# The gate of the last 256 channels of the last 128 tokens goes into their weights; the last multiplication is shared 640 to 384 by ScalarE and VectorE

## The chip, the cores and the metric

The kernel runs on one core of one Trainium2 chip, as one program. The metric is the device time of an execution in microseconds (us). The kernel before takes 963.58 us (median of 3 runs, 963.45 to 964.17). A profile is one further execution with the hardware profiler on; its timeline counts from the start of its span. Engines are TensorE (PE; PEld is its weight load), VectorE (DVE), ScalarE (ACT), GpSimd (POOL) and SyncE (SP), which issues DMA transfers.

## The reference

A decoder trunk of two layers on 1024 tokens of 1024 channels, in float32. The first layer is a gated pooling mixer. The second is sliding-window attention (16 heads of 64, window 128, one sink per head, a shared position bias) with a gate per element; its output goes through a projection `b_w_out`, is multiplied by a gate per channel (from the condition `c`) and added to the stream. A last RMSNorm follows. The change touches only the end of this:

```python
def rmsnorm(x, g):
    y = x * lax.rsqrt(jnp.mean(x * x, axis=-1, keepdims=True) + EPS)
    return y * g

# second layer; y = (o * silu(z)) @ w_out, o the attention's output
x = x + gate[:, None, :] * y
return rmsnorm(x, final_g)
```

Since the gate is one number per output channel, `gate * (a @ w)` equals `a @ (w * gate)`, up to rounding.

## The kernel before, in words

The stream is held transposed: eight tiles `x` of 128 channels by 1024 tokens. Every float32 product is made of three TensorE passes over a high and a low part of each operand (`wh`/`wl` or a pair in `raw` or `wo` for weights); a weight is split by an ACT copy (high) and a DVE subtraction (low).

The second layer (from about L1050) isn't written in the order in which it runs. Each operation is recorded by `note(engine, length, f, reads, writes, lag)` with an assumed length and lag, `in_order` (L1138) simulates the five queues with these numbers and gives the order of all engines, and the instructions are then issued in that order. The waits between engines follow from what the instructions read and write, and each engine works its queue strictly in order. `specs` (L1860 on) lists the work of TensorE: projections of queries and gates, then the output projection, per half `q` of the tokens and per group of heads; `attend` (L1328) puts the attention of a block of 128 tokens between them. An attention block goes: scores on PE (L1354, L1355) into bank `S`; on DVE a masked copy (L1358) and bias, maximum (L1365, four heads); exponentials on ACT (L1369); on DVE the reciprocal (L1376) and the product (L1378); four transposes on PE (L1388) into `tp`; high part on ACT (L1392), low part on DVE (L1393); two masks on POOL (L1400, L1404, giving `pp` and `ph`); four matmuls on PE (L1418, L1419) into `o`; ACT copy `ol` (L1425) and DVE additions (L1431), the gating (L1438) and the split of the result (L1441 on ACT, L1443 on DVE). A tile of the output projection ends on DVE with gate, residual and bank evacuation at once (L696), and then its square on ACT (L1462), summed on POOL (L1467).

The last 128 tokens of the last four heads' part are handled apart. `out_most` multiplies the other 384 tokens of the second half. The weights of that part, `wo` (four pairs, `last_w`), stay in memory. For the last tokens `out_end` (L1576 to L1578) uses the activations as the stationary operand and the weights as the moving one, so that the result has the tokens on partitions, 256 channels for each of four steps `n2`. `turn_last` transposes the stream of these tokens to match (L1553, banks `S`). `rows_in` fetches the gate along a row: SP writes the eight columns `adac[:, 40:48]` to a row in DRAM (L1530) and loads it back broadcast to all partitions (L1536); the final gain row is loaded in the same way. Both go to tiles of the ring `raw1` (two buffers, which the raw weights went through before). `add_end(n2)` then multiplies by the gate (L1592, DVE), adds the stream (L1596, DVE) into `x`, squares with a sum per token (L1599, ACT) and, for `n2` below 2, multiplies by the gain on POOL (L1603). `scale_end` takes the power −1/2 of the mean on POOL (L1622), multiplies the first 512 channels by it on ACT (L1628) and the other 512 by it and the gain on DVE (L1630), and stores each half, from ACT's queue (L1634) and SP's (L1636). The other 384 tokens are scaled by `finish` (L1744 to L1749) and stored from SP (L1753) in the same last microseconds.

## Time and profile before

| what | value |
|---|---|
| time, median of 3 runs | 963.58 us |
| profiled execution, its own time | 965.07 us |
| its span | 963.4 us |
| TensorE busy, its mean granted clock | 953.7 us (99%), 0.997 |
| DVE / ACT / POOL busy | 757.0 / 425.1 / 143.7 us |
| last matmul starts | 956.34 us |
| last stores issued, ACT and SP | 959.71 and 959.91 us |
| gate row: written (L1530), loaded (L1536) | issued at 870.40 and 884.92 us |
| gate row first read | 951.01 us (L1592) |

A row of a timeline gives start, duration, engine, line, operation, output `<-` inputs, shapes, count, and in brackets the idle time of the engine ahead of it and what ended it. The names in it are tiles of the program without buffer numbers; `raw` in a row of a profile stands for `raw1` too. A duration reaches to the result; the next instruction of the same engine can start a little before that, so what an instruction costs its engine is the distance from its start to the next one's. In a DMA row the last number is the time from issue to landing. In a table of stages each engine has its busy time and count, then come the granted TensorE clock, the DMA engines' busy share, and GB/s.

### The profile page before, as it was taken

The page shows a single profiled execution, that of the slowest core. Times are in us where ns is not written, and L with a number is a line of the kernel's source. Part 1 is how long each engine was busy: PE and PEld are TensorE (multiplying, and loading weights), DVE is VectorE, ACT ScalarE, POOL GpSimd, SP SyncE. Part 2 cuts the span into 40 slices and gives each one's busy share as a digit, 9 for nine tenths or more (in the row PEclk, how much of TensorE's full clock was granted, in tenths as well). Part 3 has the DMA queues.
Part 4 walks back from the last instruction along what each step waited for, and adds up shares of the span by engine and source line. Part 5 has one row for each costly group of instructions (what it writes and reads, how often), then busy time and mean ns, then how long its engine had stood idle before and what let it go on. Part 6 is the DMA issues. An engine that isn't in the chain of part 4 may idle for free.

```text
span 963.4 us, 12687 instructions
## 1 busy us (share of the span) xinstructions
PE 953.7 (99%) x4468; PEld 797.0 (83%) x4468; DVE 757.0 (79%) x1414; ACT 425.1 (44%) x872; POOL 143.7 (15%) x229
## 2 busy tenths in 40 slices
PE   9999999999999999999999999999999999999997
PEld 6888888888888887888888888888888888888887
DVE  6999899686978799677755659489999757678785
ACT  6536455332533344551123335366666334455434
POOL 3000000000000000000022200222222334344521
PEclk9999999999999999999999999999999999999999
DMA  9453531354125421788888725845566543448022
GB/s 347 179 176 110 197 132 44 109 184 162 48 93 192 153 66 45 265 282 311 298 303 259 259 98 173 310 150 175 188 231 242 171 148 123 167 136 185 31 88 88
DMA packets 52081, 166.57 MB, mean 173 GB/s; under 512 B 6705, under 2 KB 7857, under 8 KB 51890
## 3 DMA queue, kind: packets, MB, share of 16 engines
q1 hardware_dynamic: 39346, 119.63, 36.0%
q0 software_dynamic: 12240, 44.57, 14.2%
q10 hardware_dynamic: 432, 1.57, 0.5%
q8 instruction: 35, 0.57, 0.2%
q14 instruction: 28, 0.23, 0.1%
HBM read 129.04 MB, written 36.70 MB: 172 GB/s over the span
## 4 chain that ended last, share of the span: by engine, by line
PE 90%; DVE 6%; DMA 2%; issue 1%; ACT 0%; DVEq 0%; ACTq 0%; SPq 0%
PE ps_d L211 12%; PE ps_d L646 11%; PE ps_d L1218 9%; PE ps_d L1219 9%; PE ps_d L1220 9%; PE ps_S L211 8%; PE ps_S L646 5%; PE ps_tp L211 4%; PE ps_tp L646 3%; PE ps_o L211 3%; PE ps_o L646 2%; DVE tmp L546 2%; PE ps_d L373 2%; PE ps_S L1355 2%; PE ps_S L1354 2%; PE ps_tp L1388 1%
## 5 line engine op out<-in xcount | busy, mean ns | idle before, releaser
L211 PE MATMUL ps_d<-gh,wh 128*128 128x512 f32 x224 | 81.9, 389 | 0.0
L238 DVE CUSTOM_DVE_ANT_0 tmp<-tmp,cact,pk 128x1024 f32<-128x1024 f32 x48 | 60.8, 1282 | 24.9 <-DMA tmp<-ada_rest 24.6
L646 PE MATMUL ps_d<-hs,ws 128*128 128x512 f32 x312 | 74.9, 389 | 0.0
L1369 ACT ACTIVATE P<-P,nm 128x129 f32<-128x129 f32 x128 | 50.2, 394 | 45.5 <-DVE nm L1365 45.3
L1218 PE MATMUL ps_d<-hm,wh 128*128 128x512 f32 x176 | 69.5, 395 | 0.0
L1219 PE MATMUL ps_d<-hm,wh 128*128 128x512 f32 x176 | 68.7, 390 | 0.0
L646 PEld LDWEIGHTS ps_d<-hs,ws 128*128 128x128 f32 x312 | 58.6, 188 | 12.1
L1220 PE MATMUL ps_d<-hm,wl 128*128 128x512 f32 x176 | 68.6, 390 | 0.0
L211 PE MATMUL ps_S<-gh,wh 128*128 128x512 f32 x192 | 67.1, 390 | 0.0
L646 PE MATMUL ps_d<-ha,ws 128*128 128x512 f32 x252 | 60.5, 389 | 0.0
L616 ACT CAST ws<-tw 128x512 fp32r<-128x512 f32 x52 | 31.9, 620 | 59.4 <-DVE tw L621 19.1
L646 PEld LDWEIGHTS ps_d<-ha,ws 128*128 128x128 f32 x252 | 47.3, 188 | 9.8
L538 POOL MEMSET tmp<- 128x16 f32 x12 | 1.3, 111 | 328.6 <-DVE adac L238 122.2
L211 PEld LDWEIGHTS ps_d<-gh,wh 128*128 128x128 f32 x224 | 42.1, 188 | 8.7
L126 ACT CAST wh<-raw 128x1024 fp32r<-128x1024 f32 x24 | 25.2, 1050 | 54.0 <-PE ps_d L211 43.8
L546 DVE TENSOR_TENSOR tmp<-tmp 128x1039 f32<-128x1039 f32 (+3 forms) x36 | 44.4, 1234 | 1.0
L211 PE MATMUL ps_d<-gh,wl 128*128 128x512 f32 x112 | 43.6, 389 | 0.0
L211 PEld LDWEIGHTS ps_S<-gh,wh 128*128 128x128 f32 x192 | 35.9, 188 | 7.4
L1431 DVE SCALAR_TENSOR_TENSOR of<-ps_o,ol 64x256 f32<-64x256 f32 x64 | 26.6, 416 | 19.5 <-ACT ol L1425 18.8
L1400 POOL TENSOR_SCALAR_AFFINE_SELECT pp<-ph 128x1024 fp32r<-128x1024 f32 x28 | 30.6, 1095 | 56.8 <-DVE ph L1393 56.7
L1220 PEld LDWEIGHTS ps_d<-hm,wl 128*128 128x128 f32 x176 | 33.0, 188 | 7.1
L1218 PEld LDWEIGHTS ps_d<-hm,wh 128*128 128x128 f32 x176 | 33.1, 188 | 6.2
(354 smaller groups left out, 2632.3 us busy)
## 6 DMA issues: line engine op xcount, KB each, us to landing
tmp<-ada_rest SPq DMA_DIRECT2D x42, 512.0 KB, 4.5
raw<-wa SPq DMA_DIRECT2D x28, 512.0 KB, 3.4
raw<-wao SPq DMA_DIRECT2D x20, 512.0 KB, 5.1
raw<-kw POOLq DMA_DIRECT2D x20, 512.0 KB, 4.4
wh<-kw POOLq DMA_DIRECT2D x19, 512.0 KB, 3.6
wl<-kw POOLq DMA_DIRECT2D x19, 512.0 KB, 4.4
ad<-ada_first SPq DMA_DIRECT2D x16, 512.0 KB, 5.5
x<-xT SPq DMA_DIRECT2D x32, 256.0 KB, 5.8
```

The costliest lines, as they stand in the source:

```text
L126: nc.scalar.copy(out=wh, in_=raw)
L211: mm(p, lhs, acts(k, hl, q), start=start and k == 0 and s == 0, stop=stop and k == n - 1 and s == 2)
L238: nc.vector.tensor_tensor_reduce(out=raw, in0=raw, in1=ca, scale=0.5, scalar=pk[:, bcol:bcol + 1], op0=ALU.mult, op1=ALU.add, accum_out=ad ...
L546: nc.vector.tensor_add(out=nx[:, 2 * s - 1:], in0=cur[:, 2 * s - 1:], in1=cur[:, s - 1:PAD + T - s])
L616: nc.scalar.copy(out=ws[i][:, 0, :], in_=src)
L646: mm(ps, lhs, acts(k, hl), start=start and k == 0 and s == 0, stop=k == 3 and s == 2, skip_group_check=True)
L1218: mm(p, lh, a[0](), start=k == 0, stop=False)
L1219: mm(p, lh, a[1](), start=False, stop=False)
L1220: mm(p, ll, a[0](), start=False, stop=k == n - 1)
L1369: note(ACT, 0.41, lambda: nc.scalar.activation(pt()[:, i, :P + 1], pt()[:, i, :P + 1], AF.Exp, bias=nm()[:, i:i + 1], scale=-1.0, accum_ou ...
L1400: note(POOL, 1.12, lambda: nc.gpsimd.affine_select(out=v8(prev()), in_=v8(cur()).bitcast(F32), pattern=[[0, 8], [-1, P]], base=-1, channel ...
L1431: note(DVE, 0.36, lambda: nc.vector.scalar_tensor_tensor(out=of()[e * 64:(e + 1) * 64, :], in0=o()[0:64, es], scalar=0.5, in1=ol()[0:64, e ...
```

## The change

The raw copy of the last weight pair of the output projection (channels 768 to 1023), which was split for the 384 other tokens as before, is kept in its `raw1` tile. A new step `gate_last`, listed behind the second of the four `out_most`, multiplies it by the gate row (L1570, DVE), and splits the product into a `wl` and a `wh` tile (L1572 on ACT, L1573 on DVE). `out_end(3)` uses that pair. ACT copies the transposed stream of these 256 channels from its bank to memory (L1559), and `add_end(3)` is then one addition of the matmul's result to it (L1618). POOL multiplies channels 512 to 639 by the gain too, ACT's last multiplication takes channels 0 to 639 and DVE's 640 to 1023, and the two stores follow these borders. The gain row goes to the ring `raw`, and the squares go over the tile of the earlier squares instead of a tile of their own.

```diff
-        load("gate", rows[0], [(at, 0)])
-        load("gain", rows[1], ())
+        load("gate", rows[0], [(at, 0)], "raw1", bp, F32)
+        load("gain", rows[1], (), "raw", wp, F32R)
...
-        end["sq"] = tile_of("wh", wp, [P, 1024], F32R, 2)
+        end["sq"] = sqq[0]
...
+        u = end["u"]
+        note(ACT, 0.4, lambda: nc.scalar.copy(
+            out=u().bitcast(F32)[:, 768:], in_=end["bank", 1]()[:, 256:]),
+            [(end["bank", 1], 0)], [(u, 3)])
+
+    def gate_last():
+
+        raw, gate = end["raw"], end["gate"]
+        w = end["w"] = [whole(tile_of(t, wp, [P, 1024], F32R, 2)) for t in ("wl", "wh")]
+        row = lambda: gate()[:, 768:].rearrange("p (i c) -> p i c", i=2).unsqueeze(2).broadcast_to(
+            [P, 2, 4, P])
+        view = lambda: raw().rearrange("p (i k c) -> p i k c", i=2, k=4)
+        note(DVE, 1.2, lambda: nc.vector.tensor_mul(out=view(), in0=view(), in1=row()),
+             [(gate, 0)], [(raw, 0)])
+        note(ACT, 1.0, lambda: nc.scalar.copy(out=w[0](), in_=raw()), [(raw, 0)], w[0].on)
+        note(DVE, 1.16, lambda: nc.vector.tensor_sub(
+            out=w[1](), in0=raw(), in1=w[0]().bitcast(F32)), [(raw, 0)] + w[0].on, w[1].on)
...
-                w = last_w[n2]
+                w = last_w[n2] if n2 < 3 else end["w"]
...
+        else:
+            note(DVE, 0.45, lambda: nc.vector.tensor_add(
+                out=cut("x"), in0=ps()[:, :256], in1=cut("u")), [(ps, 0), (u, n2)], [(x, n2)])
...
-        if n2 < 2:
-            note(POOL, 0.8, lambda: nc.gpsimd.tensor_mul(
-                out=cut("u"), in0=cut("x"), in1=end["gain"]()[:, cs]),
-                [(x, n2), (end["gain"], 0), (state["rs"], 0)], [(u, n2)])
+        if n2 < 3:
+            gs = slice(cs.start, min(cs.stop, 640))
+            of = lambda name: end[name]().bitcast(F32)[:, gs]
+            note(POOL, 0.8 if n2 < 2 else 0.4, lambda: nc.gpsimd.tensor_mul(
+                out=of("u"), in0=of("x"), in1=of("gain")),
+                [(x, n2), (end["gain"], 0), (state["rs"], 0)], [(u, (n2, "a"))])
...
-        note(ACT, 0.6, lambda: nc.scalar.activation(
-            cut("u", 0), cut("u", 0), AF.Copy, scale=rs()[:, 0:1]), [(rs, 0)], [(u, 0), (u, 1)])
+        note(ACT, 0.8, lambda: nc.scalar.activation(
+            cut("u", 0, 640), cut("u", 0, 640), AF.Copy, scale=rs()[:, 0:1]), [(rs, 0)], by_act)
...
-        *[out_most(n2) for n2 in range(4)], bare(turn_last),
+        out_most(0), out_most(1), bare(gate_last), out_most(2), out_most(3), bare(turn_last),
```

The recorded order puts L1570 much earlier than its place in the list. On DVE, in the output projection some 75 us before the end, the order was before (the names are those above; L696 ends a tile of the projection):

```order
L1376 RECIPROCAL den<-den 128x4 [waits Activation_49]
L1378 TENSOR_TENSOR P<-P,den 128x4x128 [waits DVE_49]
L696 SCALAR_TENSOR_TENSOR x<-ps_d,adac,x 128x512 [waits PE_49]
L1443 TENSOR_TENSOR qt<-of,qt 128x2x128 [waits Activation_49]
L696 SCALAR_TENSOR_TENSOR x<-ps_d,adac,x 128x512 [waits PE_49]
L1358 COPY_PREDICATED ps_S<-tri,ps_S 128x2x128 [waits PE_49]
L1393 TENSOR_TENSOR ph<-ps_tp,ph 128x512 [waits Activation_49]
L1358 COPY_PREDICATED ps_S<-tri,ps_S 128x2x128 [waits PE_49]
```

and with the change:

```order
L1376 RECIPROCAL den<-den 128x4 [waits Activation_49]
L1378 TENSOR_TENSOR P<-P,den 128x4x128 [waits DVE_49]
L696 SCALAR_TENSOR_TENSOR x<-ps_d,adac,x 128x512 [waits PE_49]
L1443 TENSOR_TENSOR qt<-of,qt 128x2x128 [waits Activation_49]
L1570 TENSOR_TENSOR raw_7488<-raw_7488,raw_7604 128x1024 [waits DMAHW3_49]
L696 SCALAR_TENSOR_TENSOR x<-ps_d,adac,x 128x512 [waits PE_49]
L1431 SCALAR_TENSOR_TENSOR of<-ps_o,ol 64x256 [waits DVE_49,Activation_49]
L1358 COPY_PREDICATED ps_S<-tri,ps_S 128x2x128 [waits PE_49]
L1393 TENSOR_TENSOR ph<-ps_tp,ph 128x512 [waits Activation_49]
L1358 COPY_PREDICATED ps_S<-tri,ps_S 128x2x128 [waits PE_49]
```

L1570 (raw_7488 is the kept weight tile, raw_7604 the gate row) with its wait for the gate row's DMA stands ahead of the block's third L696 and of the next block's softmax, and one of the two L1431 has come ahead of L1358.

On SP, at the loads of the two rows (raw_7604 and raw_7612 are gate and gain), before:

```order
L1530 DMA row<-adac 128x8x1 [waits DMAHW2_49]
L1536 DMA raw_7604<-row 128x1024 [waits DMAHW2_49,DMAHW3_49,DMAHW0_49,DVE_49]
L1536 DMA raw_7612<-fg_row 128x1024 [waits DMAHW1_49,DVE_49]
L1753 DMA out<-x 128x512 [waits DMAHW5_49,DVE_49]
L1753 DMA out<-x 128x512 [waits DMAHW6_49,DVE_49]
```

and with the change:

```order
L1530 DMA row<-adac 128x8x1 [waits DMAHW2_49]
L1536 DMA raw_7604<-row 128x1024 [waits DMAHW2_49,DMAHW3_49,DMAHW0_49,DVE_49]
L1536 DMA raw<-fg_row 128x1024 [waits DMASW5_49,DMASW3_49,DMASW7_49,DMASW1_49,PE_49]
L1778 DMA out<-x 128x512 [waits DMAHW5_49,DVE_49]
L1778 DMA out<-x 128x512 [waits DMAHW6_49,DVE_49]
```

The gate's load stands where it did with the same waits; the gain's now waits for PE, the last reader of its new buffer.

On POOL, at the end of the program (wl is `u`, wh is `x`), with the change:

```order
L1731 TENSOR_TENSOR rs<-v,mhalf 128x3 [waits DVE_49]
L1626 TENSOR_TENSOR wl<-wh,raw 128x256 [waits DMASW4_49,DMAHW4_49,DVE_49,PE_49]
L1626 TENSOR_TENSOR wl<-wh,raw 128x256 [waits DVE_49]
L1626 TENSOR_TENSOR wl<-wh,raw 128x128 [waits DVE_49]
L1771 TENSOR_TENSOR x<-x,xn 128x384 [waits Activation_49]
L1645 TENSOR_TENSOR rs<-nm,mhalf 128x1 [waits DVE_49]
```

The third gain product is new and stands ahead of the 384-column product of `finish`, which was there before.

More of the change, by code (lines that the diff above doesn't have):

```diff
@@ L1626, in scale_end @@
             end["rest"](k, [(sums, 0)])
-        cut = lambda name, h: end[name]().bitcast(F32)[:, half(h)]
-        note(ACT, 0.6, lambda: nc.scalar.activation(
-            cut("u", 0), cut("u", 0), AF.Copy, scale=rs()[:, 0:1]), [(rs, 0)], [(u, 0), (u, 1)])
-        note(DVE, 0.7, lambda: nc.vector.scalar_tensor_tensor(
-            out=cut("u", 1), in0=cut("x", 1), scalar=rs()[:, 0:1], in1=end["gain"]()[:, half(1)],
-            op0=ALU.mult, op1=ALU.mult),
+        cut = lambda name, a, b: end[name]().bitcast(F32)[:, a:b]
+        by_act = [(u, (n2, "a")) for n2 in range(3)]
+        note(ACT, 0.8, lambda: nc.scalar.activation(
+            cut("u", 0, 640), cut("u", 0, 640), AF.Copy, scale=rs()[:, 0:1]), [(rs, 0)], by_act)
+        note(DVE, 0.55, lambda: nc.vector.scalar_tensor_tensor(
+            out=cut("u", 640, D), in0=cut("x", 640, D), scalar=rs()[:, 0:1],
+            in1=cut("gain", 640, D), op0=ALU.mult, op1=ALU.mult),
             [(rs, 0), (end["x"], 2), (end["x"], 3), (end["gain"], 0)], [(u, 2), (u, 3)])
-        note(ACT, 0.5, lambda: nc.scalar.dma_start(out_last[:, half(0)], cut("u", 0)),
-             [(u, 0), (u, 1)], (), 3.0)
-        note(SP, 0.35, lambda: nc.sync.dma_start(out_last[:, half(1)], cut("u", 1)),
+        note(ACT, 0.5, lambda: nc.scalar.dma_start(out_last[:, :640], cut("u", 0, 640)),
+             by_act, (), 3.0)
+        note(SP, 0.35, lambda: nc.sync.dma_start(out_last[:, 640:], cut("u", 640, D)),
              [(u, 2), (u, 3)], (), 3.0)
@@ L1668, in split_any @@
         if stays:
+            end["raw"] = raw
             t = large_tile([P, 2, T], "wo")
```

21 lines of the change are left out of this document (11 added, 10 removed).

## The prediction

> **What bounds the kernel now.** I read the page first, for the engine that carries the end.
>
> ```profile
> PE 953.7 (99%) x4468; PEld 797.0 (83%) x4468; DVE 757.0 (79%) x1414; ACT 425.1 (44%) x872; POOL 143.7 (15%) x229
> PE 90%; DVE 6%; DMA 2%; issue 1%; ACT 0%; DVEq 0%; ACTq 0%; SPq 0%
> ```
>
> TensorE is busy 99% and makes 90% of the chain that ended last. So whatever makes TensorE wait in mid-program is paid in full, and elsewhere only the few microseconds after its last matmul count. The change touches both places. The timelines of VectorE (DVE), ScalarE (ACT), GpSimd (POOL) and the SP queue show the last stage:
>
> ```profile
> 956.34 0.28 PE L1578 MATMUL ps_d<-wo,qt 128*128 128x256 f32 x1
> ...
> 956.68 0.42 DVE L1592 TENSOR_TENSOR wl<-ps_d,raw 128x256 f32<-128x256 f32 x1
> 957.13 0.42 DVE L1596 TENSOR_TENSOR wh<-ps_S,wl 128x256 f32<-128x256 f32 x1
> ...
> 958.95 0.72 ACT L1628 ACTIVATE wl<-wl,rs 128x512 f32<-128x512 f32 x1 [0.85 <-POOL rs L1622]
> ...
> 956.16 1.00 POOL L1746 TENSOR_TENSOR x<-x,xn 128x384 f32<-128x384 f32 x1 [1.34 <-ACT xn L1744]
> 958.37 0.55 POOL L1622 TENSOR_TENSOR rs<-nm,mhalf 128x1 f32<-128x1 f32 x1 [1.21 <-DVE nm L1615]
> ```
>
> After the last matmul (956.34) comes one chain: gate multiplication, residual add, square, sum, power, the two last multiplications, two stores.
>
> **The end of the program: what it gains.** For the last 256 channels the gate multiplication L1592 leaves this chain. Its start to that of L1596 is 957.13 − 956.68 = 0.45 us. The add L1618 takes its slot at 956.68 (last matmul plus 0.34, as L1592 had), so square, sum and power come 0.45 us earlier, if POOL is free. The new 128-column product of n2 = 2 stands on POOL ahead of the 384-column one that took 1.00 us from 956.16; a 256-column one took 0.74 (row below), so 128 columns are about 0.74 − 0.26 = 0.48. It can start when x is there (956.3), the next ends at 956.3 + 0.45 + 1.0 = 957.8, and the power is due at 958.37 − 0.45 = 957.92: just free.
>
> ```profile
> 954.08 0.74 POOL L1603 TENSOR_TENSOR wl<-wh,raw 128x256 f32<-128x256 f32 x1 [0.70 <-DVE wh L1596]
> ```
>
> ACT's last multiplication then starts 0.45 earlier, at 958.50, with 640 columns: 0.72 plus 128 columns at the 0.10 that lie between its 384- and 512-column rows (0.62 for L1517 below, 0.72) is 0.82, so its store issues 0.45 − 0.10 = 0.35 us earlier. VectorE's is 128 columns shorter, and SP's store issues 0.45 us and about that 0.1 earlier. The bytes of both stores together are unchanged. I take 0.4 us gained; bounds 0.2 (POOL just late) and 0.6 (all as on SP's side).
>
> **The middle: what the change adds.** L1570 multiplies the last weight tile by the gate row, on VectorE, behind the second L696 of a block of the output projection and ahead of the third. It waits for the gate row's load. The SP queue's timeline and the DMA issues show when that lands:
>
> ```profile
> 884.92 0.34 SPq L1536 DMA_DIRECT2D raw<-row  x1
> ...
> row<-adac SPq DMA_DIRECT2D x1, 4.0 KB, 14.4
> ...
> raw<-row SPq DMA_DIRECT2D x1, 512.0 KB, 7.5
> ```
>
> The write of the row takes 14.4 us, so the load issues at 884.92 and lands at 884.92 + 7.5 = 892.4. Before, nobody asked for it until 951. Now VectorE's in-order queue does, at 886.80:
>
> ```profile
> 879.62 1.23 DVE L1677 TENSOR_TENSOR wo<-raw,wo 128x1024 fp32r<-128x1024 f32 x1 [2.27 <-ACT wo L1676]
> 880.76 0.41 DVE L1431 SCALAR_TENSOR_TENSOR of<-ps_o,ol 64x256 f32<-64x256 f32 x1
> ...
> 884.00 0.75 DVE L696 SCALAR_TENSOR_TENSOR x<-ps_d,adac,x 128x512 f32<-128x512 f32 x1
> 884.66 0.41 DVE L1438 TENSOR_TENSOR of<-of,szb 128x256 f32<-128x256 f32 x1
> ...
> 885.20 0.69 DVE L1378 TENSOR_TENSOR P<-P,den 128x512 f32<-128x512 f32 x1
> 885.81 0.74 DVE L696 SCALAR_TENSOR_TENSOR x<-ps_d,adac,x 128x512 f32<-128x512 f32 x1
> 886.47 0.41 DVE L1443 TENSOR_TENSOR qt<-of,qt 128x256 fp32r<-128x256 f32 x1
> 886.80 0.74 DVE L696 SCALAR_TENSOR_TENSOR x<-ps_d,adac,x 128x512 f32<-128x512 f32 x1
> ```
>
> Queued behind L1570 are that third L696, then the whole softmax of the next block: L1431, L1358, L1393, L1365 four times, L1438, L1376, L1378. The previous block did the same in the same order, so its starts are the prices. From the landing at 892.5: L1570, 1024 columns like L1677, 1.14 (880.76 − 879.62) to 893.64; L696 0.66 to 894.30; L1431 to its second half 3.24 (884.00 − 880.76) to 897.54; L1438 and L1376 0.54 (885.20 − 884.66) and another L696 0.66 between them, to 898.74; L1378 0.69, done at 899.43. TensorE's transposes L1388 wait for that product, and L1418 waits for POOL's two masks:
>
> ```profile
> 894.87 0.39 PE L1418 MATMUL ps_o<-pp,VS 128*128 128x512 f32 x1
> ...
> 895.32 0.39 PE L1418 MATMUL ps_o<-ph,VS 128*128 128x512 f32 x1
> ...
> 895.78 0.60 PE L1388 MATMUL ps_tp<-ident,P 128*128 128x128 f32 x4
> ...
> 887.57 0.63 ACT L1462 ACTIVATE xn<-x 128x512 f32<-128x512 f32 x1 [0.36 <-DVE x L696]
> ...
> 888.29 1.30 POOL L1467 TENSOR_TENSOR rb<-rb,xn 128x512 f32<-128x512 f32 x1 [0.77 <-ACT xn L1462]
> 889.55 1.09 POOL L1400 TENSOR_SCALAR_AFFINE_SELECT pp<-ph 128x1024 fp32r<-128x1024 f32 x1
> 890.71 1.09 POOL L1404 TENSOR_SCALAR_AFFINE_SELECT ph<-ph 128x1024 fp32r<-128x1024 f32 x1
> ```
>
> POOL's masks stand behind L1467, which waits for ACT's square of the late L696: L696 done 894.38, square to 895.04, L1467 from 895.13, L1400 from 896.39 to 897.48, L1404 from 897.55 to 898.64. So TensorE stops at 894.87, gets two matmuls at 897.5, two more at 898.7, and its transposes at 899.5 instead of 895.78: **3.7 us lost**. At 897.54 VectorE's L1438 meets L1404. Where they met before, L1438 was not done until 0.28 after L1404's end:
>
> ```profile
> 853.17 1.09 POOL L1404 TENSOR_SCALAR_AFFINE_SELECT ph<-ph 128x1024 fp32r<-128x1024 f32 x1
> ...
> 853.53 1.01 DVE L1438 TENSOR_TENSOR of<-of,szb 128x256 f32<-128x256 f32 x1
> ```
>
> Then L1438 is done at 898.92 instead of 897.95, and the loss is about 4.6. The two starts are 0.01 apart; I take the middle, **4.1 us**. The lower bound comes from an earlier landing. The load waits in the DMA engines behind POOL's weight loads (q0):
>
> ```profile
> q0 software_dynamic: 178, 0.63, 100.4%
> ...
> q1 hardware_dynamic: 55, 0.20, 52.2%
> ```
>
> The first row is 886 to 888 us: q0 fills the engines for the whole stretch, and the gate (q1) begins only at its end. The second is 891 to 892. The gain load, issued 0.4 us behind it before, now waits for TensorE's last use of another tile and no longer follows it. If the gate's 512 KB go through at the second row's 0.20 MB per us with nothing else on q1, it lands near 890.5 and the loss is 3.7 − 2.0 = 1.7. I keep 892.5, since what is ahead of it in the engines is unchanged.
>
> The rest of the new work finds cover. ACT's cast L1572 (about 1.05) goes into a gap of 1.18 before the last exponentials, VectorE's subtraction L1573 (1.23) into one of 1.57, and ACT's copy of the transposed x into one of 1.61. Without the gaps 1.05 and 1.23 us of delay would stand on these two engines, ahead of the last block's softmax. The gain load, which now waits, holds up only the output stores behind it on SP's queue, and nobody waits for those before the end.
>
> ```profile
> 917.86 0.41 ACT L1369 ACTIVATE P<-P,nm 128x129 f32<-128x129 f32 x1 [1.18 <-DVE nm L1365]
> 923.38 0.75 DVE L696 SCALAR_TENSOR_TENSOR x<-ps_d,adac,x 128x512 f32<-128x512 f32 x1 [1.57 <-PE ps_d L1220]
> 949.92 0.62 ACT L1517 ACTIVATE x<-x,pk 128x384 f32<-128x384 f32 x1
> 952.15 0.42 ACT L1599 ACTIVATE wh<-wh 128x256 f32<-128x256 f32 x1 [1.61 <-DVE wh L1596]
> ```
>
> **The clock after the stall.** TensorE's timeline and the table of stages show what a thin stretch does to its clock (the column behind POOL):
>
> ```profile
> 30.35 2.12 PE L161 MATMUL ps_o<-invd,second 128*128 128x1 f32 x16 [0.44 <-DVE second L392]
> ...
> 28.50:31.90 3.40, 2.96 (x25) 2.72 (x24) 3.40 (x6) 2.21 (x5) 0.00 (x0) 1.00 0.29 117
> 31.90:35.30 3.40, 3.40 (x11) 2.82 (x11) 3.28 (x6) 0.72 (x1) 1.01 (x1) 0.50 0.00 0
> ```
>
> The 3.4 us before the drop held 25 matmuls, most of them a single column wide (the 16 of L161, two of which fall behind the drop); then 3.4 us went at half clock. A whole such stretch of dense work costs 3.4 / 2 = 1.7 us. The stall holds four matmuls in 4.6 us, thinner than that. How much of the slow stretch falls on waiting depends on where its borders lie, so the cost is 0 to 1.7; I take **1.0 us**. The Trainium skill (TensorE: Matmul & The Clock Gate, Part 1: The HAM clock gate) says that the clock halves after at least one idle window of about 3.4 us. Read strictly, the four matmuls would keep it up, since the longest unbroken wait is 2.6 us, and the sum would be 1.0 us smaller; the row speaks for the drop, since its window was not idle.
>
> **Sum.** +4.1 + 1.0 − 0.4 = +4.7 us. The profiled execution took 965.07 us (span 963.4 and 1.7 around it) and would take 969.8; the median of the runs is 1.5 lower, so 963.58 + 4.7 = **968.3 us**.
>
> **Rivals.**
> - *The clock stays up* (0.23). The same stall, 4.1 − 0.4: 967.3 us. It is what happens if only a wholly idle stretch of 3.4 us lowers the clock. For it: the four matmuls inside the stall; against it: the row at 28.50. The rule of the Trainium skill, named above, would make it the likely case.
> - *The gate row is there in time* (0.08), the case on the other side. If it lands by about 889.2, the product is ready at 889.2 + 7.0 = 896.2, the 0.4 us gained at the end pays for it, and below 888.8 nothing is lost: 963.2 us, no change. That asks for 4 us from issue to landing instead of 7.5. For it: the page's median for a weight load of this size on POOL's queue is 3.6 to 4.4 us. Against it: the engines were full until 888.
> - *The backlog passes to the next block* (0.12). ACT's second square behind the stall waits for a late L696 and stands ahead of the copy `ol` that the next block needs: L1378 899.43, L1443 0.34, L696 0.74, square 0.53, copy 0.60, so the next L1431 starts at about 901.6, some 1.2 us later than in step with TensorE (900.4). The slack there is 904.90 − 901.81 = 3.1 us:
>
> ```profile
> 901.12 0.69 DVE L1378 TENSOR_TENSOR P<-P,den 128x512 f32<-128x512 f32 x1
> ...
> 904.90 0.60 PE L1388 MATMUL ps_tp<-ident,P 128*128 128x128 f32 x4
> ```
>
>   If POOL and VectorE block each other two or three times more, at the 1.0 us of the row at 853, the slack is gone and about 1.5 us comes on top: 969.8 us.
> - *The end does not get shorter* (0.02): 968.7 us.
>
> **How the numbers follow.** Forecast 0.55, rivals as above. The lowest sum is +1.7 + 0 − 0.4, 964.9; the highest 4.6 + 1.7 − 0.2, 969.7, and 970.0 with the backlog. The range is 964.9 to 970.0. A measurement can tell 0.2%, or 1.9 us, from no change. Slower by more than that needs a loss of over 2.3 us before the gain at the end: 0.90. No change 0.08: the early landing. Faster 0.02, since the end can give 0.6 us at most.
>
> **What would show it.** In the changed profile VectorE should have an idle time of about 5 us before L1570, ended by the DMA of the row; TensorE should wait for POOL and DVE at L1418 and L1388 near 895 to 900, where it waited for nothing; the granted clock should show 0.5 in some of the 7 us behind that; the stretch from the last matmul to the end should be 0.4 us shorter. If the row lands by 889, or TensorE has slack that I don't see at L1418, the prediction is wrong.

## The result, and the profile after

The changed kernel takes 965.79 us (median of 22 runs, 964.19 to 970.51) against 964.16 us for the kernel before, run beside it: a ratio of 1.0017 with a 95% interval of 1.0009 to 1.0025. A second series gave 966.36 us against 964.70, a ratio of 1.0025 (1.0009 to 1.0042). So the change makes the kernel slower by 1.6 to 1.7 us, where 4.7 us was predicted. The 0.2% that was to tell slower from no change lies inside both intervals.

The profiled execution of the changed kernel is one of its longer ones: 968.14 us, span 966.3 us, 2.9 us longer than the span before. The timelines of VectorE, the SP queue and TensorE show the stall in the middle as the prediction drew it:

```profile
891.33 1.23 DVE L1570 TENSOR_TENSOR raw<-raw,raw 128x1024 f32<-128x1024 f32 x1 [6.86 <-DMA raw<-row]
...
870.32 0.43 SPq L1530 DMA_DIRECT2D row<-adac  x1
883.35 0.33 SPq L1536 DMA_DIRECT2D raw<-row  x1
...
896.48 0.47 PE L1418 MATMUL ps_o<-pp,VS 128*128 128x512 f32 x1 [1.53 <-ACT P L1369]
...
897.79 0.50 PE L1418 MATMUL ps_o<-ph,VS 128*128 128x512 f32 x1 [0.61 <-POOL ph L1404]
...
898.43 0.63 PE L1388 MATMUL ps_tp<-ident,P 128*128 128x128 f32 x4
```

VectorE stands 6.86 us before L1570 until the gate row has landed, TensorE waits at L1418 twice, and L1388 starts at 898.43 instead of 895.78. This execution is 0.10 us ahead of the profile before until then, so the loss is 2.8 us. The lag stays at that to the last matmul (959.02 instead of 956.34), so nothing is lost or regained behind it. The table of stages shows no drop of the clock (the column behind POOL's stays at 1.00):

```profile
893.91:897.33 3.42, 1.74 (x7) 0.83 (x5) 3.35 (x13) 2.06 (x9) 3.29 (x3) 1.00 0.00 0
897.33:900.74 3.41, 2.95 (x18) 2.50 (x19) 2.06 (x6) 2.00 (x4) 2.62 (x3) 1.00 0.02 5
```

The end of the program, in the timeline of all engines, is not shorter but longer (the first row is from the profile before, the others from the profile after):

```profile
957.48 0.15 DVE L1615 TENSOR_TENSOR nm<-nm 128x1 f32<-128x1 f32 x1
...
959.02 0.28 PE L1595 MATMUL ps_d<-wl,qt 128*128 128x256 f32 x1
959.06 0.46 POOL L1626 TENSOR_TENSOR wl<-wh,raw 128x128 f32<-128x128 f32 x1 [1.56 <-DVE wh L1614]
...
959.36 0.42 DVE L1618 TENSOR_TENSOR wh<-ps_d,wl 128x256 f32<-128x256 f32 x1
...
959.48 0.99 POOL L1771 TENSOR_TENSOR x<-x,xn 128x384 f32<-128x384 f32 x1
959.70 0.79 DVE L1638 TENSOR_TENSOR nm<-nm 128x1 f32<-128x1 f32 x1
...
960.41 0.54 DVE L1774 TENSOR_TENSOR x<-x,ps_tp 128x384 f32<-128x384 f32 x1
960.87 0.15 DVE L1638 TENSOR_TENSOR nm<-nm 128x1 f32<-128x1 f32 x1
...
961.10 0.55 POOL L1645 TENSOR_TENSOR rs<-nm,mhalf 128x1 f32<-128x1 f32 x1 [0.63 <-DVE nm L1638]
961.68 0.83 ACT L1652 ACTIVATE wl<-wl,rs 128x640 f32<-128x640 f32 x1 [1.36 <-POOL rs L1645]
...
962.54 0.33 SPq L1660 DMA_DIRECT2D last<-wl  x1
962.54 0.37 ACTq L1658 DMA_DIRECT2D last<-wl  x1
```

The gate multiplication is gone from the chain as intended: L1618 starts 0.34 us behind the last matmul. But the addition of one column, L1638 (L1615 before, 0.15 us), takes 0.79 us. It starts while POOL's 384-column product L1771 runs and gives its result only at about that product's end (959.48 + 0.99 = 960.47). POOL runs that product then because its new 128-column product stands ahead of it. The last sum (L1638 again) follows L1774 at 960.87, the power at 961.10. Counted from the start of the last matmul, both stores issue at 3.52 us; before it was 3.37 on ACT's queue and 3.57 on SP's. The last landing of a store comes 6.17 us behind the start of the last matmul, 6.05 before. It is now that of ACT's store, which has 320 KB instead of 256 (SP's, with 192 KB, has landed at 5.68); before, SP's was the last. From the start of the last matmul to the end of the span it is 7.26 us instead of 7.03, so on the prediction's own measure the end is 0.23 us longer; why 0.11 of this lies behind the last landing is not shown. The stall and the end, less the 0.10 us, make up the 2.9 us of the span.

### The profile page after: what moved, and what is told of

The parts are those of the page before. It is cut to its first block, busy times and chain, and to the rows that moved or that the text cites. A ratio compares the mean times of both kernels' runs of the same rounds, so it can differ in the third digit from the quotient of the medians.

```text
span 966.3 us, 12700 instructions
## 1 busy us (share of the span) xinstructions
PE 954.4 (99%) x4468; PEld 797.3 (83%) x4468; DVE 758.6 (79%) x1415; ACT 427.1 (44%) x874; POOL 144.0 (15%) x230
## 4 chain that ended last, share of the span: by engine, by line
PE 81%; DVE 14%; DMA 2%; issue 2%; ACT 1%; POOL 1%; POOLq 0%; DVEq 0%; ACTq 0%
PE ps_d L211 11%; PE ps_d L646 10%; PE ps_d L1218 9%; PE ps_d L1220 9%; PE ps_d L1219 9%; PE ps_S L211 8%; PE ps_S L646 5%; PE ps_tp L211 3%; PE ps_tp L646 3%; PE ps_o L211 2%; PE ps_o L646 2%; DVE tmp L546 2%; DVE ad L238 2%; PE ps_S L1355 1%; PE ps_S L1354 1%
## 5 line engine op out<-in xcount | busy, mean ns | idle before, releaser
L646 PEld LDWEIGHTS ps_d<-hs,ws 128*128 128x128 f32 x312 | 58.6, 188 | 12.2
L1431 DVE SCALAR_TENSOR_TENSOR of<-ps_o,ol 64x256 f32<-64x256 f32 x64 | 26.6, 416 | 18.6 <-ACT ol L1425 17.9
```

The source lines that it names most:

```text
L646: mm(ps, lhs, acts(k, hl), start=start and k == 0 and s == 0, stop=k == 3 and s == 2, skip_group_check=True)
L1431: note(DVE, 0.36, lambda: nc.vector.scalar_tensor_tensor(out=of()[e * 64:(e + 1) * 64, :], in0=o()[0:64, es], scalar=0.5, in1=ol()[0:64, e ...
```

## The experiments

The theory (A): the loss is VectorE's in-order wait for the gate row, so it follows the row's landing; the size in any execution is landing + 7.1 us − 895.78, where 7.1 is the 898.43 − 891.31 of the first profile, from the landing to L1388. The rivals were the added work itself, the place of L1570 in the block, a load that is late whenever it is issued, and a spread that has nothing to do with the landing. Executions differ by up to 1.6 us before the second layer already (TensorE's clock is halved for 3.4 us near 13 us in one, near 32 us in another, in neither place in a third). Where landings or starts of two executions are compared, the offset of the same matmuls of the block at 877 us is taken off; this is called the scale of the profile before.

### L1570 two blocks later (e1_later)

```diff
-            row.rearrange("n p -> p n"), adac[:, 40:48]), last_w[3][0].on, [(at, 0)], 4.0)
+            row.rearrange("n p -> p n"), adac[:, 40:48]), last_w[3][0].on, [(at, 0)], 14.4)
...
-                 on, [(t, 0)], 4.0)
+                 on, [(t, 0)], 8.0)
```

> The changed kernel with only the place of L1570 altered: the planner is told longer lags for the row's write and load, so that the product by the gate row stands two blocks later in VectorE's order (behind L1443 near 903 us), when the row has long landed. Theory A (the loss in the middle is the in-order wait for the gate row, 2.8 us of TensorE's time in the profiled run): no wait of TensorE at L1418/L1388 near 895 to 900, last matmul within 0.3 us of before's; the tail is 0.2 us longer than before's as in the changed kernel, so +0.0 to +0.4 us against before. Rival B (the added work itself, 3.4 us on VectorE and ScalarE, pushes the softmax late wherever it stands): TensorE still loses 1 us or more, and the time stays at +1.5 to +3. Rival C (the tail is really 0.4 shorter and the profile of the changed kernel shows a chance meeting): -0.4 us.

```profile
894.73 0.60 PE L1388 MATMUL ps_tp<-ident,P 128*128 128x128 f32 x4
...
902.11 1.21 DVE L1570 TENSOR_TENSOR raw<-raw,raw 128x1024 f32<-128x1024 f32 x1
```

(TensorE's and VectorE's timelines.) L1570 no longer waits, no wait of TensorE is left, and TensorE stays 1.06 us ahead of the profile before to its last matmul; L1388 at 894.73 has no wait ahead of it. 965.14 us against 964.71, ratio 1.0010 (1.0001 to 1.0019). The added work costs TensorE nothing where it stands clear of the softmax: rival B falls. The median is 0.43 us over that of the kernel before, just above what A expected; the end of the span, 7.26 us behind the last matmul's start as in the changed kernel, explains 0.23 of it.

### The row written early (e7_row_early)

```diff
-    def rows_in():
+    def row_out():
...
-            row.rearrange("n p -> p n"), adac[:, 40:48]), last_w[3][0].on, [(at, 0)], 4.0)
+            row.rearrange("n p -> p n"), adac[:, 40:48]), (), [(at, 0)], 4.0)
...
+    row_out()
     keys(0, None, rings["bank d"][2])
```

> The changed kernel with L1570 where it is, but the write of the gate row to DRAM (L1530) issued on SP many hundreds of us earlier, so that the gate load waits for nothing and lands before L1570's turn (about 886.8 us). Theory A (late landing): idle time of VectorE ahead of L1570 below 0.5 us, no wait of TensorE at L1418/L1388, +0.0 to +0.4 us against before (tail still 0.2 longer). Rival B (L1570's place in the block, 1.2 us ahead of the softmax, costs by itself): TensorE loses up to 1.2 us there, +1.0 to +1.6. Rival D (a load of 512 KB waits for the weight loads in the DMA engines whenever it is issued, so the row's write is not what made it late): landing still past 890, a stall of 2 us or more, +1.5 to +3.

The write now issues at 603 us, the gate load at 877.33, and it lands at 881.26.

```profile
884.42 1.22 DVE L1574 TENSOR_TENSOR raw<-raw,raw 128x1024 f32<-128x1024 f32 x1
...
956.96 0.79 DVE L1642 TENSOR_TENSOR nm<-nm 128x1 f32<-128x1 f32 x1
```

The product by the gate row (L1574 here) stands where the changed kernel has it, waits for nothing, and TensorE waits for nothing at 895: rival B falls, and D as it was put (a load that is late whenever it is issued). 964.98 us against 964.71, ratio 1.0004 (0.9996 to 1.0013). The addition in the tail (L1642 here) takes 0.79 us again, so that is not a chance meeting of one execution.

### The tail's addition with a scalar operand (e8_early_scalar, e2b_scalar_only)

On top of the early write of e7:

```diff
-            note(DVE, 0.15, lambda: nc.vector.tensor_add(
-                out=sums()[:, 0:1], in0=sums()[:, 0:1], in1=sums()[:, n2:n2 + 1]),
-                [(sums, n2)], [(sums, 0)])
+            note(DVE, 0.15, lambda: nc.vector.tensor_scalar(
+                out=sums()[:, 0:1], in0=sums()[:, 0:1], scalar1=sums()[:, n2:n2 + 1],
+                scalar2=0.0, op0=ALU.add, op1=ALU.add), [(sums, n2)], [(sums, 0)])
```

> As the kernel with the early row, and the last sum's addition L1638 written with the second sum as a per-partition scalar instead of a second tensor. Theory A2 (the tail lost its gain because L1638, with two SBUF tensors as inputs, was held for 0.6 us until POOL's product L1771 ended; 0.79 us instead of 0.15): L1638 takes 0.15 to 0.2 us beside a running POOL, the power L1645 still stands behind POOL's L1774 and starts 0.0 to 0.6 us earlier, the stretch from last matmul to end is 0.2 to 0.6 us shorter than in the early-row kernel, total -0.6 to -0.1 against before. Rival E (POOL's own queue, L1774 behind L1771, is what sets the power, whenever the sum is there): tail as in the early-row kernel within 0.1 us. Rival F (the form with a scalar is held by POOL as well): L1638 again 0.6 us or more.

```profile
956.69 0.99 POOL L1775 TENSOR_TENSOR x<-x,xn 128x384 f32<-128x384 f32 x1
956.90 0.20 DVE L1642 TENSOR_SCALAR nm<-nm 128x1 f32<-128x1 f32 x1
...
958.62 0.61 DVE L1658 SCALAR_TENSOR_TENSOR wl<-wh,rs,raw 128x384 f32<-128x384 f32 x1
959.30 0.35 ACTq L1662 DMA_DIRECT2D last<-wl  x1
```

And SP's queue alone:

```profile
956.68 2.84 SPq L1782 DMA_DIRECT2D out<-x  x5
959.63 0.39 SPq L1664 DMA_DIRECT2D last<-wl  x1
```

Beside a running POOL the same sum takes 0.20 us instead of 0.79. The two forms differ in the second sum: a second tensor from SBUF in the one, a scalar per partition in the other. The Trainium skill (SBUF — State Buffer, SBUF: two separate sides) says that a VectorE operation with two SBUF inputs and a GpSimd operation that reads SBUF exclude each other for the whole instruction; these rows agree. The chain now gives nearly what was predicted for it (0.35 us for ACT's store): that store issues 959.30 − 956.23 = 3.07 us behind the start of the last matmul, 0.30 us earlier than before and 0.45 earlier than in the changed kernel. Yet SP's store issues at 3.40, right where SP has issued its stores of the other tokens (956.68 + 2.84 = 959.52), though VectorE's multiplication was done at 959.23. The last landing comes at 6.11 us, against 6.17 and, before, 6.05, and the span ends at 7.08, against 7.26 and 7.03. The time is 965.17 us against 964.71, ratio 1.0006 (0.9997 to 1.0014); the −0.6 to −0.1 us that A2 expected did not come. The profile shows nothing that would make it longer than the kernel before by 0.5 us either, and the interval includes no change.

The same edit in the changed kernel with nothing else altered:

> The changed kernel with nothing altered but the form of L1638 (the second sum as per-partition scalar). One more pair of landing and stall: stall at L1388 = landing + 7.1 - 895.78 (+ 0.9 if L1438 is the one held beside L1404) on the time scale of the kernel before, none if L1570 does not wait. At the end: L1638 0.2 us beside POOL's product as in the early-row kernel with that form, ScalarE's last store issued 3.05 to 3.15 us after the start of the last matmul (3.37 before, 3.52 in the changed kernel), SP's last store 3.35 to 3.45 us after it.

Stores at 3.06 and 3.38 us, last landing at 6.09: the same tail. Its stall is in the table further down.

### Two stores less (e11_two_stores_less)

On top of the edits of e8:

```diff
                 tile(k, on)
-                store(k)
+                if k not in (5, 6):
+                    store(k)
```

This kernel leaves out two of the sixteen stores of the transposed output (192 KB each).

> The early-row kernel with the scalar form, and two of the last eight stores of the transposed output left out (k = 5 and 6, 192 KB each; that part of the output is not written), to tell what holds the last store back. In the kernel with all stores ScalarE's last store goes out 0.51 us earlier than with the tensor form, but SP's only 0.18 us, right behind SP's eight other stores, and the end comes 0.14 us earlier. Theory J (SP's queue and the bytes of these stores hold the end): SP's last store issues within 0.1 us of the end of VectorE's last multiplication (0.3 us earlier), and the stretch from the last matmul to the end is 0.3 to 1.0 us shorter than 7.07 us. Theory K (the chain of the last 256 channels alone sets the end): 7.0 to 7.1 us again.

```profile
955.86 0.28 PE L1599 MATMUL ps_d<-wl,qt 128*128 128x256 f32 x1
...
958.93 0.33 SPq L1664 DMA_DIRECT2D last<-wl  x1
958.93 0.38 ACTq L1662 DMA_DIRECT2D last<-wl  x1
```

SP's store now issues at 3.07 us together with ACT's, and the last landing comes at 5.69 us instead of 6.11. So theory J holds for the kernel with the scalar form: SP's queue or the bytes of the other stores hold its end, not the chain of the last 256 channels; this run does not tell the two apart. The span shows 0.2 us of these 0.4 (6.86 instead of 7.08), less than J expected.

### A later landing (e6_bounce)

```diff
+        row2 = kp.tile([KT, P], F32, name="row2")
+        note(SP, 0.35, lambda: nc.sync.dma_start(row2, row), [(at, 0)], [(at, 0)], 1.5)
```

> The changed kernel with one more copy of the gate row between its write and its load, from one DRAM row to another; the orders of VectorE, ScalarE, POOL and TensorE are unchanged, only the landing is later, by 2 to 4 us. Theory A (TensorE's product ready 7.1 us behind the landing): the stall grows one for one, 2.8 + 2 to 4 = 4.8 to 6.8 us, total +5 to +7 us against before in the profiled run. Rival G (the stall has slack that the first 2.8 us already used up or did not, so later stages take some up): last matmul later by less than the stall, by 1 us or more. On the clock: if half a clock follows a thin stretch of over 3.4 us, the granted clock shows 0.50 behind the stall and up to 1.7 us come on top; if not, 1.00 throughout.

```profile
890.91 1.23 DVE L1572 TENSOR_TENSOR raw<-raw,raw 128x1024 f32<-128x1024 f32 x1 [7.31 <-DMA raw<-row]
...
895.93 1.09 POOL L1404 TENSOR_SCALAR_AFFINE_SELECT ph<-ph 128x1024 fp32r<-128x1024 f32 x1
895.94 1.35 DVE L1438 TENSOR_TENSOR of<-of,szb 128x256 f32<-128x256 f32 x1
...
898.91 1.08 PE L1388 MATMUL ps_tp<-ident,P 128*128 128x128 f32 x4 [1.11 <-DVE P L1378]
```

Its table of stages:

```profile
894.80:898.21 3.41, 1.43 (x4) 0.59 (x4) 3.31 (x11) 2.22 (x10) 2.15 (x3) 1.00 0.00 0
898.21:901.63 3.42, 2.71 (x13) 2.75 (x14) 2.10 (x5) 2.19 (x4) 2.59 (x2) 0.50 0.03 5
```

On the scale of before the load is issued 5.6 us later and takes 3.6 us instead of 8.0, so it lands only 1.2 us later (892.61), less than the 2 to 4 us that were expected. TensorE loses 4.9 us at L1388: 892.61 + 7.1 − 895.78 = 3.9, and 0.93 for L1438, which starts with POOL's L1404, is held to 1.35 us, and passes that on. These are the two values between which the prediction took the middle. Then follows the clock: a stretch of 3.41 us with 1.43 us of TensorE work, then half clock for 3.41 us, which costs another 1.3 us. Four runs have a median of 971.4 us, ratio 1.0073 (1.0058 to 1.0088). Of the 2.1 us by which the stall grew, 1.2 follow the landing one for one, and the meeting on VectorE and POOL makes the rest; the clock comes on top.

### More executions of the same two kernels (after_b, after_c, after_d, before_b)

> The changed kernel once more, unaltered, for a second pair of landing and stall. Theory A (stall = landing of the gate row + 7.1 us - 895.7, on the time scale of the kernel before; one us more where VectorE's L1438 starts together with POOL's L1404 and is the one that is held): a landing of 890 us makes 1.4 us, 891 makes 2.4, 892.5 makes 3.9 to 4.8, one below 888.6 none. The times of the five rounds spread over 964.2 to 970 us as they did, and their median is 1 to 2 us over the early-row kernel's. Rival H (the run-to-run spread of the changed kernel has nothing to do with the landing): the stall is 2.6 to 2.9 us again whatever the landing is.

> A third execution of the changed kernel, unaltered, with the same rule: stall = landing + 7.1 - 895.7 us on the time scale of the kernel before. If three landings lie within 0.5 us of each other while the times differ by 2 us or more, the landing is not what spreads them.

> A fourth execution of the changed kernel. If ScalarE waits over 4 us for the second wbo load, POOL issues its two weight loads at 884 us or later, behind the gate load (882.5 to 883.4), the gate lands by 888 and L1570 does not wait, while TensorE loses 0.9 to 1.8 us a block earlier; if ScalarE waits less, POOL's loads go first (about 882), the gate lands at 891 to 892.6 and TensorE loses 2.7 to 4.9 us, 1.3 to 1.5 more with a slow clock behind it. A landing at 891 with a long wait for wbo, or at 888 with a short one, speaks against it.

> The kernel before in a second execution, to see what its own spread of times holds: a wait of ScalarE for wbo between 0.3 and 6 us, and no wait of TensorE at 895 whatever the landing of the gate row is (nobody reads it before 951). A stall at 895 us here would speak against the wait of L1570 as cause.

The table gives every execution in which SP writes the row at 868 to 870 us and VectorE, in the changed kernels, asks for it in the block at 886. Columns: ScalarE's wait for the second weight load wbo (L1676, or L1701); what TensorE loses until L1388 of the block at 886 us; the gate row's landing on the scale of before; the wait of L1570; what TensorE loses at 895 us until L1388; the half clock behind it.

| execution | wait for wbo | lost at 886 | row landed | L1570 waited | lost at 895 | clock |
|---|---|---|---|---|---|---|
| before | 3.40 | 0 | 892.5 | not read | 0 | 0 |
| before_b | 6.04 | 2.0 | 890.0 | not read | 0 | 0 |
| changed (first profile) | 0.34 | 0 | 891.4 | 6.86 | 2.8 | 0 |
| after_b | 5.08 | 1.1 | 888.3 | 0 | 0 | 0 |
| after_c | 2.49 | 0 | 892.3 | 6.33 | 4.5 | 1.5 |
| after_d | 4.47 | 0.4 | 888.5 | 0.60 | 0 | 0 |
| e2b_scalar_only | 4.17 | 0.2 | 888.8 | 1.12 | 0 | 0 |
| e6_bounce | 1.86 | 0 | 892.6 | 7.31 | 4.9 | 1.3 |
| e9_split_load | 5.86 | 1.8 | 889.2 | 0 | 0 | 0 |

In each execution of a changed kernel the landing sets the loss at 895 us, with the 0.9 us of L1438 in after_c and e6; rival H falls. (Where TensorE has lost something at 886, the block at 895 is due later by that, and it has to be taken off the landing: in e9, 889.2 − 1.8.) after_c is the execution that the prediction described, in its row landing, in the meeting (VectorE's timeline), and in the clock (the table of stages):

```profile
890.90 1.23 DVE L1570 TENSOR_TENSOR raw<-raw,raw 128x1024 f32<-128x1024 f32 x1 [6.33 <-DMA raw<-row]
...
895.94 1.34 DVE L1438 TENSOR_TENSOR of<-of,szb 128x256 f32<-128x256 f32 x1
```

```profile
895.25:898.66 3.41, 1.44 (x4) 0.59 (x4) 3.31 (x7) 2.17 (x8) 1.69 (x2) 1.00 0.00 0
898.66:902.07 3.41, 3.17 (x14) 3.10 (x15) 2.10 (x6) 1.81 (x3) 2.95 (x3) 0.50 0.03 5
```

But the landing goes with a race, of which the profile before shows one outcome only: SP's gate load or POOL's two weight loads, whichever are issued first. after_d shows the other outcome (timelines of ScalarE, SP's queue, POOL's queue, TensorE and VectorE; the last row is POOL's first load in the first profile):

```profile
878.46 1.05 ACT L1701 CAST wo<-raw 128x1024 fp32r<-128x1024 f32 x1 [4.47 <-DMA raw<-wbo]
...
882.18 0.34 SPq L1536 DMA_DIRECT2D raw<-row  x1
...
884.30 0.55 POOL L1677 DMA_DIRECT2D wh<-kw  x1
...
885.96 0.63 PE L1388 MATMUL ps_tp<-ident,P 128*128 128x128 f32 x4 [0.28 <-DVE P L1378]
...
887.40 1.23 DVE L1570 TENSOR_TENSOR raw<-raw,raw 128x1024 f32<-128x1024 f32 x1 [0.60 <-DMA raw<-row]
...
881.96 0.55 POOL L1677 DMA_DIRECT2D wh<-kw  x1
```

The wbo load comes late, so the cast L1701, VectorE's L1702 and the softmax behind it are late, and with them the masks on POOL. POOL's two weight loads stand behind those masks and issue at 884.30; in the first profile and in after_c they issue at 881.96 and 882.05. So the gate load (882.18) goes ahead of them and lands at 887.38, 5.2 us after its issue. Where POOL's loads are first, as in the first profile and after_c, it takes 8.0 and 7.9 us. Of the nine executions of the table, the gate load is first in the five with over 4 us of wait for wbo, and it (in e9 its first piece) lands 4.6 to 6.0 us after its issue; in the other four POOL's loads are first, and it takes 7.5 to 8.0 us, except in e6, where POOL's loads have 6 us of lead and it takes 3.6. No run moves POOL's loads alone, so that their order sets the landing is inferred from these nine. The row's write has a part as well: it takes 12.2 to 14.4 us in these executions, and the gate load is issued behind it. Where the gate load is first, the price is paid a block earlier instead: TensorE's loss at 886 us is the wait for wbo less 4.0 us, within 0.1 us, in all five executions with over 4 us of it.

This loss is not the change's: before_b, in which nobody reads the gate row there, has the largest one.

```profile
881.11 1.05 ACT L1676 CAST wo<-raw 128x1024 fp32r<-128x1024 f32 x1 [6.04 <-DMA raw<-wbo]
...
886.68 0.47 PE L1418 MATMUL ps_o<-pp,VS 128*128 128x512 f32 x1 [0.83 <-DVE of L1431]
...
888.61 0.63 PE L1388 MATMUL ps_tp<-ident,P 128*128 128x128 f32 x4 [0.75 <-DVE P L1378]
```

It took 967.06 us. So the kernel before has its own late executions, from the wbo load. Of the four executions of the changed kernel, the change costs nothing in the middle in the two with over 4 us of wait for wbo, and 2.8 and 6.0 us in the others.

### The gate load in two (e9_split_load)

```diff
-        load("gate", rows[0], [(at, 0)], "raw1", bp, F32)
+        g = end["gate"] = tile_of("raw1", bp, [P, 1024], F32, 2)
+        for cs, part in ((slice(768, D), 1), (slice(0, 768), 0)):
+            note(SP, 0.35, lambda cs=cs: nc.sync.dma_start(
+                g()[:, cs], rows[0][:, cs].broadcast_to([P, cs.stop - cs.start])),
+                [(at, 0)], [(g, part)], 4.0)
...
-             [(gate, 0)], [(raw, 0)])
+             [(gate, 1)], [(raw, 0)])
```

The 256 channels that L1570 needs (128 KB) are loaded first, and L1570 waits for these alone.

> The changed kernel with the gate load in two: the 256 channels that L1570 needs first (128 KB), then the other 768 (384 KB). Everything else as in the changed kernel, the row's write included. Theory A: L1570 starts as soon as the small load lands. If the weight loads on POOL's queue keep the DMA engines full until about 888 us (as in the kernel before) and the small load then takes 0.3 us for its bytes, it lands near 888.5 to 889.5: a stall of 0 to 1 us, +0.2 to +1.2 us against before. Rival I (the small load does not get through before the weight loads behind it, landing as before at 891 to 892.5): stall 2.4 to 4.8 us, +2.5 to +5.

965.68 us against 964.70, ratio 1.0010 (1.0001 to 1.0019), beside 1.0025 (1.0009 to 1.0042) for the changed kernel in the same series; the intervals overlap. The profile can't tell A from I: in this execution wbo was late by 5.86 us, POOL's loads issued at 885.59, and a whole gate load would have been in time too. Whether the smaller load helps in the other order stays open.

### What makes wbo late: the row's write (e14, e15, e16)

The write of the gate row goes out on SP right behind the two wbo loads. In the ten profiles with that order ScalarE waited 0.34 to 6.04 us for the second of them; in the kernels with the early write it did not wait. Three kernels try that without, and with, the change.

e14 is the kernel before with the early write of e7:

> The kernel before, with nothing of the change, but with the gate row's write to DRAM issued early on SP (no longer right behind the two weight loads wbo at 870 us). In the runs so far ScalarE waited 0.3 to 5.9 us for the second wbo load wherever the row's write followed it, and not at all in the three kernels with the early write; where it waited over about 4.5 us TensorE lost 0.9 to 1.8 us at L1388 of the block at 886. Theory L (the row's 1024 elements of 4 bytes hold the weight load up): no wait of ScalarE for wbo; the slower half of the times of the kernel before (965 to 966.6 us) thins out, the median 0.0 to 0.6 us lower. Theory M (chance of other traffic): a wait of 1 to 5 us as before, median within 0.2 us.

```profile
623.25 0.50 PE L1220 MATMUL ps_d<-hm,wl 128*128 128x512 f32 x1 [0.92 <-DMA wl<-kw]
```

No wait for wbo, as theory L says. But the write, issued at 603 us, now stands beside other weight loads, and TensorE waits for one of them and loses 1.2 us; e7 lost 0.4 us at the same place, and e8 and e11, with the same early write, 0.05 us or less. 965.06 us against 964.51, ratio 1.0004 (0.9995 to 1.0013). So in two of the four profiles the harm has moved, not gone.

e15 is the kernel before with the write on ScalarE's queue, in order behind the casts that use the wbo tiles:

```diff
-        note(SP, 0.35, lambda: nc.sync.dma_start(
-            row.rearrange("n p -> p n"), adac[:, 40:48]), last_w[3][0].on, [(at, 0)], 4.0)
+        note(ACT, 0.4, lambda: nc.scalar.dma_start(
+            row.rearrange("n p -> p n"), adac[:, 40:48]), last_w[3][0].on, [(at, 0)], 14.4)
...
-        ready(1, 1), bare(rows_in),
-        *[out_most(n2) for n2 in range(4)], bare(turn_last),
+        ready(1, 1), out_most(0), bare(rows_in),
+        *[out_most(n2) for n2 in range(1, 4)], bare(turn_last),
```

> The kernel before, with the gate row's write issued from ScalarE's queue, in order behind the cast of the second wbo tile (so it can no longer run beside the wbo loads), instead of on SP at 870 us. In two executions of the kernel before ScalarE waited 3.4 and 6.0 us for wbo, and in the second TensorE lost 2.0 us for it. Theory L (the row's write beside the wbo loads holds them up): wait for wbo under 0.5 us, no stall of TensorE between 875 and 900, and no harm elsewhere, as the write at 603 us had (0.3 and 1.2 us at 623); the median 0.2 to 0.8 us below that of the kernel before. Theory M (wbo is late for other reasons): waits of 1 to 6 us as before, median the same within 0.2 us. Rival N (the write now holds up POOL's last two weight loads of 882 us): a new wait of TensorE for these, 0.5 us or more.

No wait for wbo, none of TensorE from 600 us on: L again, and N falls in this execution. 964.42 us against 964.66, ratio 0.9992 (0.9981 to 1.0002), which includes no change; its highest time in 12 runs is 965.35, that of the kernel before in 23 runs of the same series 968.25. The write slows more loads than wbo: POOL's two loads into `raw`, issued at 872.92 and 873.48 us in the profile before, landed after 13.7 and 14.9 us, in e7 without the write after 3.7 and 4.9. In e15 the second of them still took 8.9 us, in e16 14.0, but nothing waited for it.

e16 has this in the changed kernel, with `gate_last` one `out_most` later, a planned lag of 6 us for the loads, and the scalar form of L1638:

> The changed kernel with the three mends together: row's write on ScalarE's queue behind the wbo casts, L1570 later in VectorE's order (planned lags of 14.4 and 6 us), and L1638 in the scalar form. Expected where all three hold: no wait of VectorE before L1570 over 0.5 us, no stall of TensorE after 875, the stretch from last matmul to the last landing of a store 6.05 to 6.15 us (6.05 before, 6.17 in the changed kernel), so the same time as the kernel before with the moved write within 0.2 us, and 1 to 2 us less than the changed kernel's median. If L1570 still waits, the stall at 895 us returns.

```profile
873.08 1.05 ACT L1701 CAST wo<-raw 128x1024 fp32r<-128x1024 f32 x1
873.54 0.39 ACTq L1530 DMA_DIRECT2D row<-adac  x1
874.03 1.05 ACT L1701 CAST wo<-raw 128x1024 fp32r<-128x1024 f32 x1
...
902.15 1.21 DVE L1570 TENSOR_TENSOR raw<-raw,raw 128x1024 f32<-128x1024 f32 x1
...
958.40 0.36 ACTq L1658 DMA_DIRECT2D last<-wl  x1
958.73 0.39 SPq L1660 DMA_DIRECT2D last<-wl  x1
```

964.06 us (963.77 to 965.32) against 964.66, ratio 0.9990 (0.9981 to 0.9999): faster than the kernel before by 0.1%, with the interval's end next to 1. The changed kernel was measured in other series; there it was 0.17 and 0.25% slower than the kernel before. (The issue of the write shows while the casts, ahead of it in ScalarE's queue, run; the second wbo load has landed at 873.51.) The last landing is 6.10 us behind the start of the last matmul, as expected. The profiles show no gain from the change's shorter chain: e15 without it has 6.06, and its median is 0.36 us higher.

## Why the prediction was right in direction and wrong in size

- **The stall of TensorE (4.1 us) was right in mechanism; its size was one case out of several.** In the first profile it is 2.8 us, with nothing for the clock and 0.2 us more at the end. The path is as drawn: L1570 behind the DMA, the softmax queued behind it, POOL's masks, L1418, L1388. The step that failed is "I keep 892.5, since what is ahead of it in the engines is unchanged". What is ahead of the gate load is a race between SP's gate load and POOL's two weight loads, and it goes either way from execution to execution: landings from 888.3 to 892.3 us on one scale in the changed kernel, and losses of 0, 0, 2.8 and 4.5 us. The 14.4 us of the row's write, taken as fixed too, was the longest that any profile shows (12.9 in the first profile of the changed kernel, which alone puts the landing some 1.5 us earlier; the load then took 0.4 us longer). And the sum of one execution was carried over to the median of all. With the landing measured, the prediction's own sum gives the loss within about 0.1 us, and after_c, which landed at 892.3, took 970.09 us, where 969.8 was predicted for a profiled execution. The rival that the row is in time got a chance of 0.08; with 4 us from issue to landing asked for, it came in two of the four executions of the changed kernel, after 4.6 and 5.2 us, and by another mechanism than the one weighed (POOL's loads came later, and the write ended earlier).
- **L1438 against L1404 (the middle of 3.7 and 4.6).** Both occur. In the first profile POOL's L1404 was the one held (1.37 us), VectorE's L1438 took 0.42; in after_c and e6 L1438 took 1.34 and 1.35.
- **The clock (1.0 us) is 0 in three of the four executions of the changed kernel and 1.5 us in after_c; in e6 it is 1.3.** It does not drop in the first profile, where TensorE was busy 1.74 us of the stretch from 893.91 to 897.33. It drops where 1.44 (after_c) and 1.43 us (e6) of 3.41 are busy. The borders of these stretches matter. Inside one execution the drops start a whole number of steps of 3.413 us apart: 278 steps between the drops at 13.28 and 962.18 us of the first profile, 19 between those at 898.66 and 963.51 us of after_c, 19 in e6. The three stretches are steps of this raster. Across two steps, from 894.95 to 898.36 us, the first profile has only 1.27 us of busy time, and its clock stayed up. So whether a stall costs the clock depends on where it falls on the raster, which is an inference from three stalls. Of the executions with a stall, the rival in which the clock stays up is right for the first profile only. The reading of the thin stretch at 28.50 us was right against the rule: the Trainium skill (TensorE: Matmul & The Clock Gate, Part 1: The HAM clock gate) asks for at least one idle window, and here four matmuls in the window did not keep the clock up. Busy time is not the whole measure: the stretch at 28.50 us had 2.96 us of it, in matmuls that are mostly one column wide. What is counted is not shown.
- **The end (−0.4 us) is +0.23 us on the span, +0.12 at the last landing.** Two steps failed. "POOL is just free" looked at POOL's queue alone: the power does wait for its input, not for POOL, but the addition that makes the input is held by POOL's product for 0.64 us. And the gain of a store's issue was taken as a gain of the end: with that mended, ACT's store issues 0.30 us earlier than before, and the last landing is 0.06 us later, because SP's queue or the bytes of the other stores end there (e11). The rival that the end doesn't get shorter, 0.02, was right about the end.
- **The backlog did not pass to the next block** in any execution; the lag behind L1388 is constant but for the half clock.
- **The upper end of the range (970.0) is no sum of its terms:** 969.7 and the backlog's 1.5 would be 971.2. Nothing measured hangs on it.
- **Cover for the other new work held.** In e1 and e16 the whole of it runs and TensorE waits for nothing.
- **The median.** The changed kernel's executions are a mixture: a wbo load that is less late, and a loss of 2.8 and 6.0 us (the clock included) at 895; or wbo later still, a loss of 0.4 and 1.1 us at 886, of the kind that the kernel before has as well, and none at 895. The four executions of the changed kernel took 968.14, 965.32, 970.09 and 964.82 us. The median of 1.6 us lies between the two groups; how often each comes is not settled by so few profiles.

## What to carry to other kernels

When an edit makes an engine wait for a transfer that nobody waited for before, the landing time in one profile is a sample, not a constant: look what else is on the queues in the microseconds around, and whose issue that depends on, and give the term a range from the one order to the other. Before counting a shorter last chain as gain, look what else leaves by the same queue at the end. A DMA of many 4-byte elements is best put where no load that matters is under way; where it stood here, the wait that came with it cost the kernel before 2.0 us in one of two profiles, more than the change could win.

## What the runs showed of the hardware that was not expected

- A write of 1024 elements of 4 bytes took 12 to 14.4 us from issue to landing, and ScalarE waited 0.3 to 6.0 us for the 512 KB load issued just ahead of it in ten of ten profiles; without the write behind it there was no such wait in six of six. Why 4 KB do this is not shown.
- An addition of two single columns took 0.79 us on VectorE beside POOL's product of two SBUF tensors, 0.15 us alone, and 0.20 us beside it with the second column as a scalar operand.
- Two instructions that start within 0.01 us of each other on VectorE and POOL: either may be the one that is held (L1404 1.37 us with L1438 0.42; L1438 1.35 with L1404 1.09).
- The drops of TensorE's clock lasted 3.41 us inside the program and started whole steps of 3.413 us apart. After a step with 42% of it busy the clock dropped (after_c, e6), after one with 51% it did not (first profile); but before the drop at 31.92 us 87% was busy, with mostly one-column matmuls, so the share alone is not the rule.
